# Weight rings in small blocks, sums of weights by transfers alone, and one more pair of seven products, in an encoder block

## The chip, the cores and the metric

The kernel runs on one core of a Trainium2 chip. The metric is the device time of one execution in microseconds. Engines are named as in the profile: PE (TensorE, with PEld its weight loads), DVE (VectorE), ACT (ScalarE), POOL (GpSimd) and SP (SyncE, which here only issues DMAs).

## The reference, cut to what matters

One layer of a bidirectional encoder over 256 tokens of width 2048, in float32:

```
h = rms_norm(x);  q, k, v of two attention branches, gates ga, gb = split(h @ w_in)
ya = windowed attention (8 query heads);  yb = dilated attention (12 heads in 3 groups, merged to 4)
merged = sigmoid(ga) * (ya @ w_branch_a) + sigmoid(gb) * (yb @ w_branch_b)
x = x + merged @ w_out
hf = rms_norm(x);  g = depthwise_conv3(hf @ w_ffn_gate)
x = x + (gelu(g) * (hf @ w_ffn_up)) @ w_ffn_down          # inner width 5632
x = x + sigmoid(rms_norm(x) @ w_ple_gate) * (p @ w_ple_proj)
out = rms_norm(x)
```

Nearly all of the work is the weight matrices, about 270 MB that are read once.

## The kernel before, in words

**Weights.** The weights lie in HBM as 258 pieces in the order of their use (`_pieces`), each 128 partitions by 16 blocks of 128 columns (1 MB). A piece goes by DMA on SP's queue into one of three `raw` buffers (`load`, L251). `produce` (L293) then splits a unit of it, mostly eight blocks (1024 columns), into two float32r parts: ACT copies it to `hi` (L310) and DVE subtracts, `lo = raw - hi` (L311). The parts stand in a ring of six buffers of eight blocks (`u`) or, for units that hold sums of weights, in a second ring of two (`v`). `drop` gives a buffer back when PE has used it, and `pump` produces the next units as long as a buffer is free. PE multiplies high and low parts in three passes (`thirds`, L413 to L415) or, where features are the output's partitions, in a 512-column and a 256-column pass (L356, L363).

**Stages.** A projects queries, keys and values and does the attention. B0 to B3 are the gates, each followed by the two branch projections `ba`, `bb`. D0 and D1 are the output projection. Then the MLP in two halves: E0 (gate and up), F00 and F01 (down), and the same as E1, F10 and F11. Last come the small projection `pp` and the gate G0, G2, G3. PE's program order follows the stages; a scheduler may move single instructions where nothing pins them.

**Quads.** B, D, F and G0 are made of pairs of 128-row chunks times two 512-column halves, for both 128-token halves (`quad_stage`, L420). A pair of kind `s` takes eight products of three matmuls each. Kinds `Z` and `S` take seven (Strassen's scheme in Winograd's form): PE accumulates M1 to M7 in seven PSUM banks, and DVE adds them up at a stage's end (`row_sums`, L910; the adds are L918 to L921). Seven products need four sums of the weights' quarters and four sums of the activations. The patterns are strings by stage: `GATES` for B0 to B3, `OUTS` for D, `DOWN` for the halves of F, `ALT` for G0.

For an `S` piece DVE makes all four sums of weights in the raw buffer (L289 and the two lines after it). For a `Z` piece one of the four is made ahead (`sum_ahead`, L263), in two halves of 256 columns: POOL's queue loads three quarters into spare space in SBUF (L269), DVE adds twice (L272, L273), POOL's queue stores the sum to HBM (L276). The piece is later loaded as three quarters (L255) and that sum (L256), and DVE makes the other sums (L283, L284). The stages' sums were spread by hand: 20 pieces for B and D in A (with spare space in the bias buffer `hb`), 12 for F0 in E0, 14 for F1 and G0 in E1. The DVE adds and POOL's transfers are pinned to program order (`keep`).

**Other names.** `rr` (L537) is the power on POOL that ends a norm's mean square; it stands in front of A's and of E0's sums in POOL's queue and near the end. `xr` holds the residual rows. L1016 multiplies a branch's sums into the gates, L998 takes the gates.

Of the kernel before, what the change touches and what calls it, by code (L numbers as in the profile page):

```python
# [2 lines left out]

# [165 lines left out]
def _unit_list():  # L169

    units, of = [], []
    for p, (kind, _) in enumerate(_PIECES):
        if p == 0:
            cuts = [("n", a * P, b * P) for a, b in ((0, 1), (1, 4), (4, 7), (7, 11), (11, PIECE))]
        elif kind == "Z":
            cuts = [("n", WIDE, 2 * WIDE), ("n", 2 * WIDE, 4 * WIDE), ("T21", 0, 2 * WIDE), ("T03", 2 * WIDE, 4 * WIDE)]
# [18 lines left out]
def _encoder(ctx: ExitStack, tc, xt, pt, xrow, cols, gainrow, table, onehot, mask, ident_in, wts, out):  # L195
# [55 lines left out]
    def load(r, a=0, b=PIECE):  # L251
        if a == 0:
            raws[r] = wpool.tile([P, PIECE * P], F32, name="raw", bufs=3)
        if _PIECES[r][0] == "Z":
# [1 line left out]
            nc.sync.dma_start(raws[r][:, :WIDE], ahead.pop(r))  # L256
# [4 lines left out]
    ahead = {}

    def sum_ahead(p, h, tag):  # L263

# [4 lines left out]
        keep(nc.gpsimd.dma_start(q, wts[p][:, :3 * WIDE].rearrange("p (q c) -> p q c", c=WIDE)[:, :, cols]))  # L269

        def add():
            keep(nc.vector.tensor_tensor(q[:, 0], q[:, 2], q[:, 0], op=ALU.subtract))  # L272
            keep(nc.vector.tensor_tensor(q[:, 0], q[:, 0], q[:, 1], op=ALU.add))  # L273
# [6 lines left out]
    def sums_of_weights(raw):  # L280

        q = [raw[:, i * WIDE:(i + 1) * WIDE] for i in range(4)]
        nc.vector.tensor_tensor(q[1], q[0], q[1], op=ALU.subtract)  # L283
        nc.vector.tensor_tensor(raw[:, 2 * WIDE:], raw[:, 2 * WIDE:], view(q[0], 0, (0, 2), (1, WIDE)), op=ALU.subtract)  # L284

    def all_sums_of_weights(raw):

        q = [raw[:, i * WIDE:(i + 1) * WIDE] for i in range(4)]
        nc.vector.tensor_tensor(raw[:, :2 * WIDE], raw[:, WIDE:3 * WIDE], raw[:, :2 * WIDE], op=ALU.subtract)  # L289
        nc.vector.tensor_tensor(q[2], q[2], q[0], op=ALU.subtract)  # L290
# [1045 lines left out]
```

## Time and profile before

| | us |
|---|---|
| median of three runs | 1455.06 (1453.43 to 1455.11) |
| profiled execution, its own time | 1453.29 |
| its span, first to last instruction | 1451.5 |
| PE busy | 1439.8 |
| DVE busy | 1255.9 |
| ACT busy | 836.3 |
| POOL busy | 126.7 |

The mean granted TensorE clock is 0.998. In the rows that follow, a group's row ends in its busy time, the mean duration of one instruction in ns and, behind the bar, the idle time of its engine just before them with what ended most of it. In a timeline a row has its start and its length in microseconds, and in brackets the idle time before it. A matmul's end is modelled and overlaps the next one's start, so the pace of PE is read from starts. In a DMA queue's row stand its packets, the MB moved, and the time of its packets as a share of 16 DMA engines; q1 is the queue that SP feeds, q0 that of POOL.

### The profile page before, as it was taken

The page shows a single profiled execution, that of the slowest core. Times are in us where ns is not written, and L with a number is a line of the kernel's source. Part 1 is how long each engine was busy: PE and PEld are TensorE (multiplying, and loading weights), DVE is VectorE, ACT ScalarE, POOL GpSimd, SP SyncE. Part 2 cuts the span into 40 slices and gives each one's busy share as a digit, 9 for nine tenths or more (in the row PEclk, how much of TensorE's full clock was granted, in tenths as well). Part 3 has the DMA queues.
Part 4 walks back from the last instruction along what each step waited for, and adds up shares of the span by engine and source line. Part 5 has one row for each costly group of instructions (what it writes and reads, how often), then busy time and mean ns, then how long its engine had stood idle before and what let it go on. Part 6 is the DMA issues. An engine that isn't in the chain of part 4 may idle for free.

```text
span 1451.5 us, 20060 instructions
## 1 busy us (share of the span) xinstructions
PE 1439.8 (99%) x7455; PEld 1231.0 (85%) x7455; DVE 1255.9 (87%) x1827; ACT 836.3 (58%) x1160; POOL 126.7 (9%) x193
## 2 busy tenths in 40 slices
PE   9999999999999999999999999999999999999997
PEld 8888888888888888788888888888888888888885
DVE  8778776779999999989787899997878799898994
ACT  7455544546656656666555566565545466564863
POOL 0112222210000000000222000000222200000000
PEclk9999999999999999999999999999999999999999
DMA  9776677764456466475777655566777765556462
GB/s 334 274 286 240 227 259 261 255 223 174 177 207 227 172 228 235 170 262 216 272 253 256 240 208 189 198 251 220 256 278 254 276 239 200 198 187 243 163 232 87
DMA packets 67805, 331.17 MB, mean 228 GB/s; under 512 B 8628, under 2 KB 13620, under 8 KB 41340
## 3 DMA queue, kind: packets, MB, share of 16 engines
q1 hardware_dynamic: 52268, 280.46, 53.7%
q0 software_dynamic: 14720, 48.25, 9.2%
q8 instruction: 58, 0.95, 0.3%
q10 hardware_dynamic: 720, 1.19, 0.2%
q14 instruction: 39, 0.32, 0.1%
HBM read 315.67 MB, written 14.20 MB: 227 GB/s over the span
## 4 chain that ended last, share of the span: by engine, by line
PE 92%; DVE 3%; issue 2%; DMA 1%; ACT 0%; POOL 0%; POOLq 0%; SPq 0%; DVEq 0%; ACTq 0%
PE bank L356 28%; PE bank L363 15%; PE bank L413 13%; PE bank L414 13%; PE bank L415 13%; PE bank L340 2%; PE bank L402 1%; PE bank L404 1%; PE bank L403 1%; PE bank L341 1%; DVE ul L311 1%; PE bank L966 1%; DMA raw<-in_wts 1%; DVE vl L311 1%; DMA xr<-in_xrow 0%
## 5 line engine op out<-in xcount | busy, mean ns | idle before, releaser
L310 ACT ACTIVATE uh<-raw 128x1024 fp32r<-128x1024 f32 (+2 forms) x519 | 515.4, 1007 | 293.1 <-PE bank L415 88.8
L311 DVE TENSOR_TENSOR ul<-raw,uh 128x1024 fp32r<-128x1024 f32 (+2 forms) x519 | 590.7, 1157 | 63.5 <-ACT uh L310 42.6
L356 PE MATMUL bank<-hf,uh 128*128 128x512 f32 x1408 | 336.6, 391 | 0.0
L356 PEld LDWEIGHTS bank<-hf,uh 128*128 128x128 f32 x1408 | 258.8, 188 | 50.6 <-DVE hf L522 0.4
L363 PEld LDWEIGHTS bank<-hf,ul 128*128 128x128 f32 x1408 | 180.7, 191 | 7.0
L363 PE MATMUL bank<-hf,ul 128*128 128x256 f32 x1408 | 183.3, 283 | 0.0
L310 ACT ACTIVATE vh<-raw 128x1024 fp32r<-128x1024 f32 x106 | 111.0, 1055 | 56.1 <-DVE raw L283 29.9
L311 DVE TENSOR_TENSOR vl<-raw,vh 128x1024 fp32r<-128x1024 f32 x106 | 127.3, 1217 | 1.7 <-ACT vh L310 0.5
L356 PE MATMUL bank<-hs,uh 128*128 128x512 f32 x432 | 103.6, 392 | 0.0
L356 PEld LDWEIGHTS bank<-hs,uh 128*128 128x128 f32 x432 | 79.5, 188 | 15.6
L414 PE MATMUL bank<-ul,act 128*128 128x512 f32 x218 | 84.8, 389 | 0.0
L415 PE MATMUL bank<-uh,act 128*128 128x512 f32 x218 | 84.8, 389 | 0.0
L413 PE MATMUL bank<-uh,act 128*128 128x512 f32 x218 | 84.5, 389 | 0.0
L505 ACT ACTIVATE t<-bank 128x256 f32<-128x256 f32 x122 | 45.4, 375 | 60.8 <-PE bank L363 50.1
L269 POOL DMA_DIRECT2D ahead<-in_wts x52 | 38.8, 747 | 378.5 <-DMA ahead<-ahead 209.3
L1112 ACT ACTIVATE gw<-gw,cl 128x256 f32<-128x256 f32 x44 | 24.1, 594 | 71.5 <-DVE gw L1109 71.4
L413 PE MATMUL bank<-uh,hs 128*128 128x512 f32 x154 | 60.8, 395 | 0.0
L272 DVE TENSOR_TENSOR ahead<-ahead 128x256 f32<-128x256 f32 x52 | 21.9, 422 | 44.7 <-DMA ahead<-in_wts 44.6
L415 PE MATMUL bank<-uh,hs 128*128 128x512 f32 x154 | 60.1, 390 | 0.0
L414 PE MATMUL bank<-ul,hs 128*128 128x512 f32 x154 | 60.0, 389 | 0.0
L363 PE MATMUL bank<-hs,ul 128*128 128x256 f32 x432 | 56.6, 284 | 0.0
L284 DVE TENSOR_TENSOR raw<-raw 128x1024 f32<-128x1024 f32 x46 | 56.0, 1217 | 0.3
(270 smaller groups left out, 2526.1 us busy)
## 6 DMA issues: line engine op xcount, KB each, us to landing
raw<-in_wts SPq DMA_DIRECT2D x205, 1024.0 KB, 4.9
raw<-in_wts SPq DMA_DIRECT2D x46, 768.0 KB, 4.6
ahead<-in_wts POOLq DMA_DIRECT2D x52, 384.0 KB, 5.1
hb<-in_wts POOLq DMA_DIRECT2D x40, 384.0 KB, 5.0
raw<-ahead SPq DMA_DIRECT2D x46, 256.0 KB, 4.9
ahead<-ahead POOLq DMA_DIRECT2D x52, 128.0 KB, 4.5
raw<-in_wts SPq DMA_DIRECT2D x12, 512.0 KB, 6.7
ahead<-hb POOLq DMA_DIRECT2D x40, 128.0 KB, 3.1
```

Of the source, the lines that this page charges most:

```text
L269: keep(nc.gpsimd.dma_start(q, wts[p][:, :3 * WIDE].rearrange("p (q c) -> p q c", c=WIDE)[:, :, cols]))
L284: nc.vector.tensor_tensor(raw[:, 2 * WIDE:], raw[:, 2 * WIDE:], view(q[0], 0, (0, 2), (1, WIDE)), op=ALU.subtract)
L310: nc.scalar.activation(hi, src, AF.Copy)
L311: nc.vector.tensor_tensor(lo, src, hi.bitcast(F32), op=ALU.subtract)
L340: nc.tensor.matmul(acc, hi[:, w], m, start=first, stop=False, skip_group_check=True)
L356: nc.tensor.matmul(acc, weights(u)[0][:, o * P:(o + 1) * P], m, start=first, stop=False, skip_group_check=True)
L363: nc.tensor.matmul(acc[:, T:], weights(u)[1][:, o * P:(o + 1) * P], m[:, :T], start=False, stop=last, skip_group_check=True)
L413: nc.tensor.matmul(acc, sh, wh, start=first, stop=False)
L414: nc.tensor.matmul(acc, sh, wl, start=False, stop=False)
L415: nc.tensor.matmul(acc, sl, wh, start=False, stop=last)
L505: keep(nc.scalar.activation(t, acc[:, T:], AF.Copy, scale=scale))
L1112: nc.scalar.activation(c[:, i], g[:, i], AF.Identity, scale=tap(1, f), bias=tap(3, f))
```

## The change

The three raw buffers become one tile of 48 blocks, and the two rings of split weights one queue of single blocks, first in first out: 48 blocks in the first store (`w`) and, from the end of the attention on, 16 more in a second (`v`). Loads are a list of steps of about half a piece, each issued as soon as enough blocks have been given back (`feed`), in groups of four at a time. A unit that does not lie in one run of blocks is split, and summed, run by run.

All `S` pieces become `Z`. A `Z` piece is now loaded as two sums from HBM (8 blocks) and three quarters (12 blocks), 20 blocks instead of 16. The two sums are made by four transfers between places in HBM on POOL's queue, two of which add while they write: quarter 0 is copied, quarter 1 added to it; the result is copied, quarter 3 added to that. DVE adds nothing for them and makes the other two sums in SBUF. The order of the seven products changes (M5 and M6, then M1, M2, M3, then M7, M4), with some signs. The steps for B are spread over A's jobs, those for D over B1 to B3, those for F and G0 over E0 and E1. In the second half of F the pattern has six `Z` in eleven instead of five. The ring of PSUM banks in E starts at another place.

The core of the diff (left out: signs, names, the list of first loads):

```diff
-GATES = ("sssssSSs", "ZsZZsSZs", "ZsZSsSZs", "ZsZSsSZs")
+GATES = ("sssssZZs", "ZsZZsZZs", "ZsZZsZZs", "ZsZZsZZs")
-DOWN = ("ZZsZsZsZsZs", "ZsZsZsZsZss")
-LASTS = 34
-ASK, ADD, STORE = 0, 12, 13
+DOWN = ("ZZsZsZsZsZs", "ZsZZsZsZsZs")
...
-            cuts = [("n", WIDE, 2 * WIDE), ("n", 2 * WIDE, 4 * WIDE), ("T21", 0, 2 * WIDE), ("T03", 2 * WIDE, 4 * WIDE)]
+            cuts = [(0, 8, 4), (8, 20, 8), (8, 16, 20)]
...
-RINGS = {"u": 6, "v": 2}
+STORE = {"w": 48, "v": 16}
+RAW = 48
...
+    def feed():
+        while state["load"] < len(loads):
+            step = loads[state["load"]]
+            if callable(step):
+                step()
+            else:
+                p, a, b = step
+                if len(rawfree) < b - a:
+                    break
+                if _PIECES[p][0] != "Z":
+                    load(p, a, b, wts[p][:, a * P:b * P])
+                elif a == 0:
+                    assert adding.pop(p) == 0
+                    load(p, a, b, ahead.pop(p))
+                else:
+                    load(p, a, b, wts[p][:, WIDE:])
+            state["load"] += 1
...
-        keep(nc.gpsimd.dma_start(q, wts[p][:, :3 * WIDE].rearrange("p (q c) -> p q c", c=WIDE)[:, :, cols]))
-        def add():
-            keep(nc.vector.tensor_tensor(q[:, 0], q[:, 2], q[:, 0], op=ALU.subtract))
-            keep(nc.vector.tensor_tensor(q[:, 0], q[:, 0], q[:, 1], op=ALU.add))
-        def store():
-            keep(nc.gpsimd.dma_start(ahead[p][:, cols], q[:, 0]))
+        def step(dst, src, op):
+            keep(nc.gpsimd.dma_start(dst, src, accum_op=op))
+            adding[p] -= 1
+        adding[p] = 4
+        return [partial(step, *e) for e in ((two, q[0], ALU.bypass), (two, q[1], ALU.add),
+                                            (three, two, ALU.bypass), (three, q[3], ALU.add))]
...
-        nc.vector.tensor_tensor(q[1], q[0], q[1], op=ALU.subtract)
-        nc.vector.tensor_tensor(raw[:, 2 * WIDE:], raw[:, 2 * WIDE:], view(q[0], 0, (0, 2), (1, WIDE)), op=ALU.subtract)
+        for o, op in ((8, ALU.subtract), (12, ALU.add)):
+            three, q = (runs_of(raws[p][i:i + 4]) for i in (4, o))
+            assert len(three) == len(q) == 1
+            three, q = (rawt[:, r[0][1] * P:(r[0][1] + 4) * P] for r in (three, q))
+            nc.vector.tensor_tensor(q, three, q, op=op)
...
+        cuts = sorted({r[2] for r in made[u][0]} | {r[2] for r in runs_of(raws[p][a:b])} | {b - a})
+        for o, e in zip(cuts, cuts[1:]):
+            hi, lo = part_of(u, o, e - o)
+            src = rawt[:, raws[p][a + o] * P:(raws[p][a + o] + e - o) * P]
+            nc.scalar.activation(hi, src, AF.Copy)
+            nc.vector.tensor_tensor(lo, src, hi.bitcast(F32), op=ALU.subtract)
...
-                    todo = (("M1", m1, 0, 0, 0), ("M7", sums[2], 2, 1, None), ("M6", sums[1], 2, 0, 2),
-                            ("M5", sums[0], 3, 0, None), ("M4", m4, 3, 1, 3),
-                            ("M2", m2, 1, 1, None), ("M3", sums[3], 1, 0, 1))
+                todo = (("M5", sums[0], 0, 0), ("M6", sums[1], 0, 1),
+                        ("M1", m1, 1, 0), ("M2", m2, 1, 1), ("M3", sums[3], 1, 2),
+                        ("M7", sums[2], 2, 0), ("M4", m4, 2, 1))
...
+    def spread_sums(pieces, slots):
+        last = len(slots) - 7
+        for e, p in enumerate(pieces):
+            first = e * last // max(len(pieces) - 1, 1)
+            for n, step in enumerate(sum_ahead(p)):
+                at(slots[first + 2 * n], step)
...
+    spread_sums(summed("B0", "B1", "B2", "B3"), slots[:-3])
+    spread_sums(summed("D0", "D1"), [("B%d" % j, i, 0) for j in range(1, 4) for i in range(8)])
...
-        turns["e"] = 0
-        todo = [(p, h) for p in sevens(half) for h in range(2)]
+        turns["e"] = 5 if half else 2
+        spread_sums(summed("F10", "F11", "G0") if half else summed("F00", "F01"),
+                    [(stage, i, 0) for i in range(1, len(jobs) - joint)])
```

More of the change, by code (lines that the diff above doesn't have):

```diff
@@ L280, in sums_of_weights @@
[L280 to L290, printed above, removed]
-        nc.vector.tensor_tensor(q[3], q[3], q[2], op=ALU.subtract)
+    made, taken, raws, left_of = {}, {}, {}, {}
@@ new lines, in _encoder, with extend, runs_of @@
+    state = {"unit": 0, "at": 0, "early": True, "load": 0}
+    store, free = {}, deque()
+    rawt = wpool.tile([P, RAW * P], F32, name="raw")
+    rawfree = deque(range(RAW))
+    loads = []
+    ahead, adding = {}, {}
+    def extend(which, pool):
+        store[which] = [pool.tile([P, STORE[which] * P], FR, name=which + half) for half in ("h", "l")]
+        free.extend((which, b) for b in range(STORE[which]))
+    extend("w", wpool)
+    def runs_of(blocks):
+        runs = []
+        for o, b in enumerate(blocks):
+            which, b = b if isinstance(b, tuple) else ("raw", b)
+            if runs and runs[-1][0] == which and runs[-1][1] + runs[-1][3] == b:
+                runs[-1][3] += 1
+            else:
+                runs.append([which, b, o, 1])
+        return runs
@@ new lines, in sum_of_weights, with part_of @@
+    def sum_of_weights(p):
+        for o, op in ((8, ALU.subtract), (12, ALU.add)):
[3 more added lines that the diff above has]
+            nc.vector.tensor_tensor(q, three, q, op=op)
+    def part_of(u, o, n):
+        runs, gone = made[u]
+        which, b, first, size = next(r for r in runs if r[2] <= o < r[2] + r[3])
+        assert gone <= o and o + n <= first + size
+        a = (b + o - first) * P
+        return [t[:, a:a + n * P] for t in store[which]]
@@ L308, in produce @@
-        hi = pool.tile([P, b - a], FR, name=ring + "h", bufs=RINGS[ring])
-        lo = pool.tile([P, b - a], FR, name=ring + "l", bufs=RINGS[ring])
-        nc.scalar.activation(hi, src, AF.Copy)
-        nc.vector.tensor_tensor(lo, src, hi.bitcast(F32), op=ALU.subtract)
-        if behind and u == _UNITS_OF[p][1]:
-            (sums_of_weights if _PIECES[p][0] == "Z" else all_sums_of_weights)(raw)
-        made[u] = (hi, lo)
+        p, a, b, done = _UNITS[u]
+        feed()
+        taken[u] = deque(free.popleft() for _ in range(b - a))
@@ L322, in pump, with weights, drop @@
                 break
             produce()
-    def weights(u):
+    def weights(u, o, n=1):
         while state["unit"] <= u:
             produce()
-        return made[u]
-    def drop(u):
-        del made[u]
-        state["u" if _UNITS[u][1] == "n" else "v"] += 1
+        return part_of(u, o, n)
+    def drop(u, n=None):
+        n = n or len(taken[u])
+        free.extend(taken[u].popleft() for _ in range(n))
+        made[u][1] += n
+        if not taken[u]:
+            del made[u], taken[u]
@@ L442, in cut @@
         def cut(u, i):
[L443 removed]
+            return weights(u, 4 * i, 4)
         for i, p in enumerate(pieces):
```

177 lines of the change are left out of this document (59 added, 118 removed).

## The prediction

> **What bounds the kernel now.** I read the page's totals first, then the busy time of each engine by stage, then the starts of single matmuls.
>
> ```profile
> span 1451.5 us, 20060 instructions
> PE 1439.8 (99%) x7455; PEld 1231.0 (85%) x7455; DVE 1255.9 (87%) x1827; ACT 836.3 (58%) x1160; POOL 126.7 (9%) x193
> ```
>
> PE is bound. By stage (columns: window, its length, then busy time and count of PE, PEld, DVE, ACT, POOL, the clock, the DMA share, GB/s), in the order A, B, D, first up and gate stage (E0), first down stage (F0), E1, F1:
>
> ```profile
> 60.00:320.00 260.00, 259.65 (x1469) 227.84 (x1468) 201.16 (x353) 135.79 (x219) 51.41 (x78) 1.00 0.72 257
> 330.00:545.00 215.00, 215.00 (x960) 176.83 (x959) 211.53 (x268) 132.48 (x153) 0.00 (x0) 1.00 0.55 201
> 545.00:625.00 80.00, 79.67 (x357) 64.65 (x356) 79.25 (x95) 51.58 (x63) 0.00 (x0) 1.00 0.60 211
> 640.00:860.00 220.00, 220.00 (x1266) 194.40 (x1264) 184.10 (x306) 124.84 (x186) 30.20 (x46) 1.00 0.70 246
> 870.00:990.00 120.00, 120.00 (x545) 99.38 (x544) 113.47 (x125) 68.29 (x77) 1.52 (x2) 1.00 0.59 217
> 1000.00:1225.00 225.00, 225.00 (x1296) 198.86 (x1295) 189.39 (x314) 126.30 (x187) 35.49 (x54) 1.00 0.69 247
> 1230.00:1340.00 110.00, 110.00 (x490) 90.97 (x489) 98.55 (x110) 64.45 (x74) 0.00 (x0) 1.00 0.57 212
> ```
>
> Between 60 and 1340 us PE shows 0.7 us idle (0.35 in A, 0.33 in D). DVE is the second engine: 98% busy in B, 99% in D, 95% in F0, but only 77 to 84% in A and in the E stages, where most of the adds for sums made ahead stand. So work taken from DVE pays only where DVE makes PE wait. A busy matmul overlaps the next, so small waits are read from starts. In D:
>
> ```profile
> 580.98 0.39 PE L415 MATMUL bank<-uh,merged 128*128 128x512 f32 x1
> ...
> 581.66 0.39 PE L415 MATMUL bank<-uh,merged 128*128 128x512 f32 x1
> 581.89 0.39 PE L413 MATMUL bank<-vh,S 128*128 128x512 f32 x1
> 582.58 0.50 PE L413 MATMUL bank<-vh,S 128*128 128x512 f32 x1 [0.30 <-DVE c L919]
> ```
>
> Three matmuls, one product of a quad, start 0.68 us apart (580.98 to 581.66), 0.227 each; 581.89 to 582.58 is 0.69 instead, so 0.46 us was lost to DVE. The other named wait is in A:
>
> ```profile
> 109.70 3.37 PE L356 MATMUL bank<-hs,uh 128*128 128x512 f32 x14
> 113.41 0.39 PE L711 MATMUL bank<-near,v 128*128 128x256 f32 x1 [0.35 <-DVE near L770]
> ```
>
> ```profile
> 108.93 0.42 DVE L272 TENSOR_TENSOR hb<-hb 128x256 f32<-128x256 f32 x1 [0.51 <-DMA hb<-in_wts]
> ```
>
> Fourteen matmuls at 0.227 end at 112.9, the next starts at 113.41: 0.5 us, with DVE having stood 0.51 us before it at an add whose data had not landed.
>
> **PE work.** Two pairs go from eight products to seven, one in each second-half down stage: 2 x 0.68 = **-1.36 us**. The seven S pieces that become Z stay at seven products. This term has no cover; PE is the bound.
>
> **DVE work.** Durations by shape:
>
> ```profile
> L311 DVE TENSOR_TENSOR ul<-raw,uh 128x1024 fp32r<-128x1024 f32 x461 | 554.5, 1218 | 60.7 <-ACT uh L310 40.1 <-issue 14.0 <-PE bank L363 6.1
> L284 DVE TENSOR_TENSOR raw<-raw 128x1024 f32<-128x1024 f32 x46 | 56.0, 1217 | 0.3
> L311 DVE TENSOR_TENSOR ul<-raw,uh 128x512 fp32r<-128x512 f32 x54 | 36.9, 683 | 1.5 <-ACT uh L310 1.5
> L283 DVE TENSOR_TENSOR raw<-raw 128x512 f32<-128x512 f32 x46 | 31.4, 684 | 0.3
> L272 DVE TENSOR_TENSOR ahead<-ahead 128x256 f32<-128x256 f32 x52 | 21.9, 422 | 44.7 <-DMA ahead<-in_wts 44.6
> L273 DVE TENSOR_TENSOR ahead<-ahead 128x256 f32<-128x256 f32 x52 | 21.6, 415 | 0.0
> L273 DVE TENSOR_TENSOR hb<-hb 128x256 f32<-128x256 f32 x40 | 16.8, 421 | 0.7
> L272 DVE TENSOR_TENSOR hb<-hb 128x256 f32<-128x256 f32 x40 | 16.8, 419 | 6.4 <-DMA hb<-in_wts 6.4
> ```
>
> Gone: the adds of L272 and L273 (77.1 us), the sums of L283 and L284 (87.4), and those of seven S pieces (one 1024 and two 512 wide each, 7 x 2.59 = 18.1). New: 110 sums 512 wide (75.2). The residues (`lo`) are cut where a ring wraps: 710 instructions for 621 in the built programs; a second half of a 1024 costs 2 x 683 - 1218 = 0.148 us more, 13 us; two pieces have 12 blocks more, 3 us. Net about -91 us of 1255.9. In B: ten Z at 1.90 - 1.37 and seven S at 2.59 - 1.37 give 5.3 + 8.5 = 13.8 us of 211.5, so DVE falls from 98 to about 92%. What that gives PE: the A wait goes with the adds that blocked DVE (-0.5). Of the 0.46 in D I take half (-0.2), since another bank is then waited for (below). Waits too short to show as idle, in D and at the head of E0, I put at -0.5, between 0 and -2. ACT issues 97 more instructions; even at a whole 0.63 us each,
>
> ```profile
> L310 ACT ACTIVATE uh<-raw 128x512 fp32r<-128x512 f32 x54 | 34.1, 631 | 51.7 <-DMA raw<-in_wts 17.2 <-PE bank L415 13.1 <-issue 12.3
> ```
>
> they are 61 us on an engine that is idle 38% or more of each window above.
>
> **The sums by transfers.** On POOL's queue at the start of stage A, before (`hb` is the staging space, `ahead` the stored sum):
>
> ```order
> L537 TENSOR_TENSOR rr<-rv,mhalf 128x4
> L269 DMA hb<-in_wts 128x3x256 x2
> L276 DMA ahead_628<-hb 128x256
> L269 DMA hb<-in_wts 128x3x256
> L276 DMA ahead_628<-hb 128x256
> ```
>
> and now (numbers are the pieces' sums):
>
> ```order
> L566 TENSOR_TENSOR rr<-rv,mhalf 128x4
> L306 DMA ahead_488<-in_wts 128x512
> L306 DMA ahead_489<-in_wts 128x512
> L306 DMA ahead_488<-in_wts 128x512
> L306 DMA ahead_489<-in_wts 128x512
> L306 DMA ahead_490<-in_wts 128x512
> L306 DMA ahead_488<-ahead_488 128x512
> ```
>
> Load, DVE add and store become four transfers a piece that wait only for one another. No engine paces them: POOL runs 108 of them (27 pieces, B and D) as fast as they land once its first power is done, and 112 (28 pieces) once its second, at E0's head, is. Their prices:
>
> ```profile
> q1 hardware_dynamic: 52268, 280.46, 53.7%
> ...
> ahead<-in_wts POOLq DMA_DIRECT2D x52, 384.0 KB, 5.1
> ahead<-ahead POOLq DMA_DIRECT2D x52, 128.0 KB, 4.5
> ```
>
> ```profile
> L256 SPq DMA_DIRECT2D raw<-ahead x46: 326/383/1393, 344.4 to 1371.5; - x46
> L537 POOL TENSOR_TENSOR rr<-rv,mhalf x3: 721/1018/1086, 53.1 to 1361.0; 128x2 f32<-128x2 f32 x2, 128x4 f32<-128x4 f32 x1
> ```
>
> The main queue moves 1 MB in 0.537 x 1451.5 / 280.46 = 2.78 us of all 16 DMA engines. A piece's four transfers write 1.05 MB and read 1.57 MB (an add reads its target too): 2.9 us of DMA if only the writes count, 4.4 if the reads do. No row shows an adding transfer; below 2.9 nothing argues for a gain. I take 4.4. One transfer lands in 4.5 to 5.1 us by the rows nearest in size, and each waits for the third before it, so one ends every 1.5 to 1.7 us: 108 are done 162 to 184 us after 54, by 240, and the first sum is loaded at 344. The 112 from 638 are done by 830; F0 begins at 870. So nothing waits for a sum: **0**. The cover is that distance; in A it holds for all 108 up to 2.7 us each.
>
> Raw loads share the DMA engines: 1.05 MB per 5.57 us in A and E is 2.92 us, 52%; 27 x 4.4 us in 186 us add 64%. That is over 100%, so sums spread out rather than raw loads, if raw loads are not held back. Two stretches of the DMA queues in A speak for that: POOL issued a load at 103.27, and from 103 to 106 the queues show
>
> ```profile
> q1 hardware_dynamic: 131, 0.98, 83.0%
> q0 software_dynamic: 12, 0.05, 4.0%
> ```
>
> ```profile
> 103.27 0.74 POOL L269 DMA_DIRECT2D hb<-in_wts  x1 [2.90 <-DMA ahead<-hb]
> ```
>
> The raw load, already in hand, went first and whole. [...]
>
> **Rings.** Raw loads of 1 MB become halves freed in blocks of four: earlier in A and E. A Z piece holds 20 raw blocks instead of 16, 0.26 MB x 55 = 14.4 MB more (5%), and its second load waits until its predecessors free 12. Split blocks of both stores form one queue of 64, where a quarter piece used to hold a whole buffer. These I set against each other: 0, between -1 and +2.
>
> **The order on PE.** A Z piece now begins with M5, whose bank DVE reads last at a stage's end; the scheduler moves it back. On PE where the first branch stage (`yb`, ending in M5's bank) meets the next quad stage, before:
>
> ```order
> L415 MATMUL bank_3682<-uh_3590,yb_3305 128x512
> L413 MATMUL bank_3721<-uh_3620,hs_95 128x512
> L414 MATMUL bank_3721<-ul_3621,hs_95 128x512
> L415 MATMUL bank_3721<-uh_3620,hs_95 128x512
> L413 MATMUL bank_3729<-vh_3636,S_3482 128x512
> ```
>
> and now (3332 is the branch's M5; 3373 is M6, 3380 M1, 3369 the new M5):
>
> ```order
> L450 MATMUL bank_3332<-wh_92,yb_3000 128x512
> L448 MATMUL bank_3373<-wh_92,S_3154 128x512
> L449 MATMUL bank_3373<-wl_93,S_3154 128x512
> L450 MATMUL bank_3373<-wh_92,S_3154 128x512
> L448 MATMUL bank_3380<-wh_92,hs_98 128x512
> L449 MATMUL bank_3380<-wl_93,hs_98 128x512
> L450 MATMUL bank_3380<-wh_92,hs_98 128x512
> L966 MATMUL bank_3384<-ident_75,c_3209 128x128
> L448 MATMUL bank_3391<-wh_92,hs_98 128x512
> L448 MATMUL bank_3369<-wh_92,S_3154 128x512
> ```
>
> M1 led and M5 came later still; M5 now comes seven matmuls and a transpose in, about 1.7 us after the branch's last. DVE's read in the trace:
>
> ```profile
> 367.10 0.39 PE L415 MATMUL bank<-uh,yb 128*128 128x512 f32 x1
> ```
>
> ```profile
> 370.55 0.68 DVE L1016 SCALAR_TENSOR_TENSOR c<-c,bank 128x512 f32<-128x512 f32 x1
> ```
>
> ```profile
> 583.64 0.68 DVE L921 TENSOR_TENSOR c<-bank,c 128x512 f32<-128x512 f32 x1
> ```
>
> M5 was free at 371.23, 3.9 us after the branch ended at 367.33: DVE was behind. With the same lag PE would lose 2.2 us here, and at D's middle 1.1 (free at 584.32; M5 now third there, 581.89 + 1.36 = 583.25) for the 0.46 before. With DVE at 92% instead of 98 a stage of some 57 us gives back about 3.5 us of lag, so I put the boundaries at 0.
>
> **Sum.** -1.36 - 0.5 - 0.2 - 0.5 = -2.56 us. The profiled execution took 1453.29 us (span 1451.5 and 1.8 around it); the median of the three runs is 1455.06, 1.8 above it. Taken from the median: **1452.5 us**. A measurement of this kernel can tell a change of about 0.2% (2.9 us) from none, so the forecast lies just inside that.
>
> **Rivals.**
> *The waits move to M5's bank.* DVE keeps its lag, since more blocks in one queue let it run further into work that is not urgent. Then 2.2 us at the first branch and 0.6 more in D, and about 0.5 at each of five like boundaries (three branches, two down stages): -2.36 + 2.2 + 0.6 + 2.5 = +2.9, 1458 us. For it: DVE's 3.9 us above; against it: 91 us less work.
> *Contention, slower.* The unpaced transfers hold raw loads back in A after 54 us and in E0 after 638. Raw needs 52%; it decides from the point where POOL takes more than 48% for longer than the three pieces in the raw ring (16.7 us of PE work) cover. If raw gets 45%, a piece takes 2.92 / 0.45 = 6.5 us instead of 5.57 over 27 x 4.4 / 0.55 = 216 us, so 33 pieces x 0.92 = 30 less 16.7, 14 us, twice: +28 - 2, 1481 us. For it: no engine paces POOL, and the price of an adding transfer is unseen. Against it: the raw load that went first at 103.27, and a DMA share of 0.72 in A now without a wait on raw that PE shows.
> *All small waits go.* DVE is never late again in B, D and F: the hidden waits give 3 instead of 0.5 and D its whole 0.46: -5.3, 1449.8 us.
> That the transfers make no sums ahead at all is no rival: the program holds 220 of them.
>
> **How the numbers follow.** Forecast 0.56 (between -1 and -4.5, which splits into 0.31 faster by more than 0.2% and 0.25 within it), small waits gone 0.08 (faster), waits at M5 0.20 (0.13 within, 0.07 slower), contention 0.16 (slower): faster 0.39, same 0.38, slower 0.23. The range goes from 1449 (all small waits) to 1465 (waits at M5, and the first third of contention); above it I leave about 0.1, below it 0.06.
>
> **What would show it.** Right: 5,003 matmuls of 512 columns and no change of the 0.227 us step; DVE near 1165 us; no idle at 113 and less than 0.5 us around 582; POOL's transfers over by about 240 and 830 us; PE not waiting for raw weights in A or E0. Wrong: PE idle in A beyond 0.35 us with ACT waiting for raw loads that land later than 8 us after issue (contention); PE released by the DVE lines that read M5 (L921, L1016) for a microsecond or more at stage starts (waits moved); sums that land so late that SP stands before a load from `ahead`.

## The result, and the profile after

The changed kernel took 1510.12 us (median of 4 runs, 1507.16 to 1513.6) beside 1454.24 us of the kernel before on the same chip: a ratio of 1.0385, 95% interval 1.0359 to 1.0412, so 3.9% slower. The forecast was 1452.5 us with a range of 1449 to 1465. The totals of the page of the changed kernel:

```profile
span 1506.4 us, 20758 instructions
PE 1458.2 (97%) x7449; PEld 1236.3 (82%) x7449; DVE 1183.6 (79%) x1741; ACT 856.0 (57%) x1257; POOL 157.3 (10%) x229
```

PE has the six matmuls less that were forecast (7449 for 7455), DVE is 72 us lighter, and the span is 55 us longer. By stage (columns as in the prediction; A, then D with E0's head, E0, F0):

```profile
60.00:320.00 260.00, 255.92 (x1436) 224.96 (x1435) 170.97 (x265) 131.16 (x214) 71.49 (x104) 0.99 1.00 281
545.00:640.00 95.00, 88.30 (x383) 69.62 (x382) 79.72 (x100) 52.54 (x68) 0.00 (x0) 0.98 0.64 218
640.00:860.00 220.00, 216.68 (x1235) 189.95 (x1235) 174.64 (x293) 134.35 (x222) 43.85 (x63) 1.00 0.93 264
870.00:1010.00 140.00, 124.13 (x538) 99.10 (x537) 97.69 (x122) 64.41 (x78) 31.63 (x46) 0.94 0.92 260
```

PE, which stood idle for 0.7 us between 60 and 1340 us before, now stands idle in A, around D's end, a little in E0 and above all in F0. The DMA share is 1.00 in A (0.72 before) and 0.92 in F0 (0.59 before). In D it is only 0.64, and PE stands idle there too: one cause alone will not do. PE's own pauses, from its timeline (start, length, in brackets the idle time and its releaser):

```profile
111.72 1.52 PE L391 MATMUL bank<-hs,wh 128*128 128x512 f32 x6
117.33 0.58 PE L719 MATMUL bank<-near,v 128*128 128x256 f32 x1 [4.08 <-DVE near L778]
...
592.31 0.39 PE L450 MATMUL bank<-wh,merged 128*128 128x512 f32 x1
596.02 0.50 PE L448 MATMUL bank<-wh,S 128*128 128x512 f32 x1 [3.32 <-DVE c L921]
...
597.53 0.63 PE L450 MATMUL bank<-wh,merged 128*128 128x512 f32 x1
597.96 0.63 PE L448 MATMUL bank<-wh,S 128*128 128x512 f32 x1
...
964.66 0.40 PE L450 MATMUL bank<-wh,ends 128*128 128x512 f32 x1
969.34 0.80 PE L448 MATMUL bank<-wh,S 128*128 128x512 f32 x1 [4.28 <-ACT wh L339]
```

The place that lost 0.46 us before (D0 to D1) now loses 3.5 (592.31 to 596.02, less 0.227). After the pause the matmuls start 0.43 us apart instead of 0.227 (597.53 to 597.96), and the clock column of the windows says why:

```profile
597.20:600.20 3.00, 3.00 (x9) 2.32 (x8) 3.00 (x4) 1.23 (x2) 0.00 (x0) 0.50 1.03 427
972.00:979.00 7.00, 6.25 (x15) 4.41 (x15) 7.00 (x12) 3.34 (x4) 1.65 (x2) 0.50 0.97 245
```

The granted clock is 0.50 there. The trace's clock records show half the clock for 27.3 us in all between 60 and 1400 us, and for none of the kernel before in that time; the 60 matmuls started in these stretches that did not also wait took 9.2 us more than their usual steps. The stretches last 3.41, 6.83 and 10.24 us. In the 3.41 us from 112.32 us PE was busy for 0.92 us, in those from 593.61 us for 1.00 us, and a stretch at half the clock began behind both; in the 3.41 us from 433.20 us it was busy for 1.84 us, and the clock stayed at 1.00.

To add pauses up I take, for each matmul, the time to the next one's start less 0.227, 0.120 or 0.109 us by its shape, and count what is over 0.04 us (slow matmuls of a halved clock are in it), over the whole execution. That gives 12.3 us before and **67.9 us after**. 1451.5 - 1.4 for the products + 55.6 = 1505.7 us, and the span is 1506.4: the pauses are the whole loss.

What ACT and DVE waited for, before and then after:

```profile
ACT uh L310 <- DMA raw<-in_wts: 54.3, 46, 5.1
```

```profile
ACT wh L339 <- DMA raw<-in_wts: 96.2, 59, 9.2
...
ACT vh L339 <- DMA raw<-in_wts: 29.9, 14, 3.8
...
DVE wl L340 <- ACT wh L339: 115.7, 88, 8.4
```

Raw data is late (126 us of waiting for 54), and DVE stands at `lo` behind ACT (115.7 us, 42.6 before). PE's own longest waits, after:

```profile
PE bank L449 <- DVE wl L340: 8.2, 7, 1.6
PE bank L448 <- ACT wh L339: 7.4, 5, 4.3
PE bank L448 <- DVE c L921: 5.5, 3, 3.3
PE bank L719 <- DVE near L778: 4.1, 1, 4.1
```

So PE stands first of all for the split weights themselves (L340, L339); the adds that it also waits for (L921, L778) are queued behind splits on DVE. The DMA queues between 60 and 300 us, before and after:

```profile
q1 hardware_dynamic: 7709, 43.13, 51.0%
q0 software_dynamic: 5841, 19.14, 21.6%
...
raw<-in_wts SPq DMA_DIRECT2D x38, 1024.0 KB, 5.0
```

```profile
q0 software_dynamic: 10800, 25.27, 50.9%
q1 hardware_dynamic: 13324, 42.05, 49.2%
...
raw<-in_wts SPq DMA_DIRECT2D x74, 512.0 KB, 8.4
ahead<-in_wts POOLq DMA_DIRECT2D x74, 256.0 KB, 8.8
```

With both queues busy each took about half of the time there (between 700 and 830 us, in E0, it is 55.0% for q1 and 41.3% for q0), a raw load of half the size landed in 8.4 us for 5.0, and a sum's transfer in 8.8 us. So POOL's transfers end late. On POOL's timeline stand the last of A's, one pair of E0's (the last for F0 and the first for F1) and the very last:

```profile
324.58 0.81 POOL L306 DMA_DIRECT2D ahead<-in_wts  x1 [5.49 <-DMA ahead<-ahead]
...
823.59 1.36 POOL L306 DMA_DIRECT2D ahead<-in_wts  x2 [5.33 <-DMA ahead<-ahead]
...
988.04 0.80 POOL L306 DMA_DIRECT2D ahead<-in_wts  x1 [6.56 <-DMA ahead<-ahead]
```

Their last packets end at 330 us in A and at 994 us after E0. Yet no load waited for a sum: no row of SP's waits names a transfer that writes `ahead`.

### The profile page after: what moved, and what is told of

The parts are those of the page before. It is cut to its first block, busy times and chain, and to the rows that moved or that the text cites. A ratio compares the mean times of both kernels' runs of the same rounds, so it can differ in the third digit from the quotient of the medians.

```text
span 1506.4 us, 20758 instructions
## 1 busy us (share of the span) xinstructions
PE 1458.2 (97%) x7449; PEld 1236.3 (82%) x7449; DVE 1183.6 (79%) x1741; ACT 856.0 (57%) x1257; POOL 157.3 (10%) x229
## 4 chain that ended last, share of the span: by engine, by line
PE 39%; DMA 7%; DVE 6%; issue 2%; ACT 1%; POOL 0%; POOLq 0%; DVEq 0%; ACTq 0%
PE bank L391 20%; PE bank L398 11%; DMA raw<-in_wts 7%; DVE wl L340 3%; PE bank L448 3%; PE bank L449 3%; PE bank L450 3%; ACT wh L339 1%; DVE vl L340 1%; DVE raw L318 1%; DMA raw<-ahead 1%; PE bank L966 0%; ACT vh L339 0%; DVE c L919 0%; DVE xr L1033 0%
## 5 line engine op out<-in xcount | busy, mean ns | idle before, releaser
L340 DVE TENSOR_TENSOR wl<-raw,wh 128x1024 fp32r<-128x1024 f32 (+3 forms) x546 | 576.6, 1080 | 199.9 <-ACT wh L339 115.7
L339 ACT ACTIVATE wh<-raw 128x1024 fp32r<-128x1024 f32 (+3 forms) x546 | 506.9, 944 | 369.5 <-PE bank L391 118.7
L391 PE MATMUL bank<-hf,wh 128*128 128x512 f32 x1056 | 256.5, 391 | 1.3 <-DVE c L921 1.3
L391 PEld LDWEIGHTS bank<-hf,wh 128*128 128x128 f32 x1056 | 194.1, 188 | 39.2 <-DVE c L921 1.7
L340 DVE TENSOR_TENSOR vl<-raw,vh 128x512 fp32r<-128x512 f32 (+2 forms) x174 | 155.5, 911 | 26.3 <-ACT vh L339 16.2
L339 ACT ACTIVATE vh<-raw 128x512 fp32r<-128x512 f32 (+2 forms) x174 | 136.2, 804 | 59.2 <-DMA raw<-in_wts 29.9
L398 PEld LDWEIGHTS bank<-hf,wl 128*128 128x128 f32 x1056 | 137.0, 191 | 5.2
L398 PE MATMUL bank<-hf,wl 128*128 128x256 f32 x1056 | 140.8, 283 | 0.0
L391 PE MATMUL bank<-hs,wh 128*128 128x512 f32 x432 | 103.6, 392 | 0.0
L448 PE MATMUL bank<-wh,act 128*128 128x512 f32 x209 | 82.9, 399 | 1.8 <-ACT wh L339 1.7
L450 PE MATMUL bank<-wh,act 128*128 128x512 f32 x209 | 82.6, 395 | 0.0
L448 PE MATMUL bank<-wh,S 128*128 128x512 f32 x118 | 48.8, 415 | 12.6 <-ACT wh L339 5.7
```

Source lines behind the costliest of these rows:

```text
L339: nc.scalar.activation(hi, src, AF.Copy)
L340: nc.vector.tensor_tensor(lo, src, hi.bitcast(F32), op=ALU.subtract)
L391: nc.tensor.matmul(acc, weights(u, o)[0], m, start=first, stop=False, skip_group_check=True)
L398: nc.tensor.matmul(acc[:, T:], weights(u, o)[1], m[:, :T], start=False, stop=last, skip_group_check=True)
L448: nc.tensor.matmul(acc, sh, wh, start=first, stop=False)
L450: nc.tensor.matmul(acc, sl, wh, start=False, stop=last)
```

## The experiments

Two causes suggested themselves: contention (C) and the rings with the order on PE (R). All ratios are to the kernel before, on the same chip; "pauses" are summed as above, in the one execution that was profiled (in e1 and e11 the slowest, 5 and 9 us above the median). The rows come from several chips, on which the kernel before took 1454.1 to 1455.6 us, and the four runs of e9 alone go from 1472.2 to 1480.9 us. So a difference between two rows holds to some 2 to 4 us.

| kernel | us | ratio, 95% interval | pauses |
|---|---|---|---|
| the change | 1510.12 | 1.0385 [1.0359, 1.0412] | 67.9 |
| e1 no transfers | 1484.28 | 1.0194 [1.0175, 1.0214] | 49.0 |
| e2 copies only | 1498.19 | 1.0303 [1.0288, 1.0318] | 57.4 |
| e3 bb's second bank M4 | 1513.82 | 1.0411 [1.0395, 1.0426] | 75.3 |
| e4 E1's transfers held | 1498.04 | 1.0304 [1.0278, 1.0331] | 49.2 |
| e5 = e1, 16 raw blocks more | 1458.94 | 1.0026 [1.0016, 1.0036] | 19.3 |
| e6 = e1, 8 split blocks less | 1485.29 | 1.0210 [1.0191, 1.0229] | 45.5 |
| e7 = e1, other banks | 1484.60 | 1.0200 [1.0183, 1.0217] | 44.2 |
| e8 = e1, 16 of 20 blocks loaded | 1476.04 | 1.0142 [1.0120, 1.0164] | 36.6 |
| e9 change, 16 raw blocks more | 1478.91 | 1.0152 [1.0125, 1.0179] | 38.5 |
| e10 = e9, E1's transfers held | 1475.19 | 1.0135 [1.0112, 1.0158] | 28.5 |
| e11 = e10, yet more raw | 1474.94 | 1.0123 [1.0094, 1.0152] | 35.3 |
| e12 before, one pair more | 1463.98 | 1.0062 [1.0042, 1.0083] | 23.5 |
| e13 = e10, padded tiles | 1471.71 | 1.0117 [1.0103, 1.0132] | 24.4 |
| e14 = e9, paced transfers | 1471.98 | 1.0120 [1.0105, 1.0134] | 31.5 |
| e15 change, paced transfers | 1498.55 | 1.0305 [1.0287, 1.0323] | 56.4 |
| e16 before, the pair later | 1464.53 | 1.0069 [1.0057, 1.0081] | 24.3 |
| e17 = e14, no tile moved | 1468.03 | 1.0092 [1.0077, 1.0107] | 28.9 |
| e18 = e9, unused tiles | 1482.90 | 1.0197 [1.0179, 1.0214] | 33.7 |

Five of these sums by stage (A from 60 to 325 us, B to 545, D to 640, E0 to 865, F0 to 1010; a slow kernel's stages begin some us late in them):

| kernel | A | B | D | E0 | F0 | rest |
|---|---|---|---|---|---|---|
| before | 2.5 | 1.3 | 2.5 | 0.3 | 0.3 | 5.4 |
| the change | 8.4 | 4.9 | 11.3 | 5.0 | 26.4 | 11.9 |
| e1 | 1.9 | 9.5 | 15.2 | 6.1 | 3.4 | 12.9 |
| e5 | 1.9 | 3.6 | 5.6 | 1.1 | 0.0 | 7.1 |
| e17 | 1.8 | 14.0 | 4.0 | 2.7 | 0.0 | 6.4 |

**Transfers taken away, made cheaper, held back.** e1 leaves the transfers out (a Z piece's first eight blocks then come from the weights, so its sums are others than the reference's):

```diff
     def spread_sums(pieces, slots):
+        return
...
-                    load(p, a, b, ahead.pop(p))
+                    load(p, a, b, wts[p][:, :2 * WIDE])
```

> The rings, the patterns and the order of the change, but POOL makes no sums: the first two blocks of four of a Z piece are loaded straight from the weights, so SP's traffic and all work on DVE, ACT and PE stay and only the 220 transfers are left out (the sums are then not the reference's). Theory C (contention: the transfers hold raw loads back in A, in E0 and in F0): the 26 us that PE loses between 916 and 1010 us, the 6 us in A and most of the 16 us between 596 and 670 go; 1465 to 1472 us. Theory R (rings and order: 20 raw blocks for a Z piece of 48, and M5's bank first): the losses stay where they are; 1500 us or more.

e2 makes the adding transfers plain copies (the adds are left out):

```diff
-        ... (two, q[1], ALU.add), ... (three, q[3], ALU.add)
+        ... (two, q[1], ALU.bypass), ... (three, q[3], ALU.bypass)
```

> All 220 transfers stay, but the 110 that add are plain copies (the sums are then not the reference's). Theory C with the price in the adding: a piece's four transfers cost about 3.1 us of DMA instead of 5.1, the last of E0's come before F0 begins, and the loss in F0 shrinks from 26 us to under 8; 1482 to 1490 us. Theory C with the price in the number of transfers and their landing: under 6 us of gain, 1504 us. Theory R: no change, 1510 us.

e4 lets POOL wait, ahead of the transfers for F1 and G0, for values of `xr` that F0 writes last:

```diff
+        if half:
+            g = sc.tile([P, 2], F32, name="hold_on", bufs=1)
+            keep(nc.vector.tensor_scalar(g, xr[:, :, D - 1], 0.0, 1.0, op0=ALU.mult, op1=ALU.add))
+            h = sc.tile([P, 2], F32, name="held_on", bufs=1)
+            keep(nc.gpsimd.tensor_tensor(h, g, mhalf[:, :2], op=ALU.pow))
         spread_sums(summed("F10", "F11", "G0") if half else summed("F00", "F01"),
```

> The 64 transfers for F1 and G0 wait on POOL for a power of a value that DVE takes from the residual rows after F0's end, so that they run in E1 and none runs in F0. Theory C: PE's loss in F0 (26 us) falls to under 5 and E1 takes the transfers without loss, 1484 to 1488 us. Theory R: the loss in F0 stays, 1508 to 1512 us.

e1 came out between the theories: the transfers cost 26 us, and 30 us stay without any. By stage the transfers' part lies in F0 and in A; in E0, where they run from 668 us on, the pauses are no fewer without them. Of the 26 the adding itself is 12 (e2, whose time lies in none of its three ranges). With the hold F0 is nearly clear of pauses:

```profile
870.00:1010.00 140.00, 137.36 (x641) 113.03 (x640) 114.35 (x145) 78.07 (x96) 0.00 (x0) 1.00 0.59 199
```

PE is busy for 137.4 of 140 us there (124.1 in the change), at a DMA share of 0.59. So transfers that run into F0 do harm there; but e4 gained only 12 us where its pauses fell by 18.7, which stayed unexplained until e18.

**The order on PE.** e3 gives the second branch stage M4's bank in place of M5's; e7 turns the banks in D1, F01 and F11, so that M5, which now comes first, uses the bank that is read first.

```diff
-  ("bb%d" % j, yb.get, ("M7", "M5"))
+  ("bb%d" % j, yb.get, ("M7", "M4"))
```

> The second branch sum stands in M4's bank instead of M5's, so that the bank that DVE frees last at a branch's end is the one that the next stage needs last. Theory R: the 1.25 us at 376 and the 2.1 us at 433 to 436 go, 1506 to 1507 us. Theory C: DVE is late there because weights were late, and PE waits a little later for the weights instead; 1509 to 1510 us.

```diff
+        turn = {"M5": "M1", "M1": "M7", "M7": "M5"} if stage in ("D1", "F01", "F11") else {}
...
-                accs[name] = bank(name)
+                accs[name] = bank(turn.get(name, name))
```

> The kernel without transfers (1484.28 us) with other PSUM banks in D1, F01 and F11: M5 there uses the bank of M1 (read first at a stage's end), M1 that of M7, M7 that of M5. O (order) expects the waits on L921 at 596, 960 and 1320 us to go with the slow matmuls behind them: 1472 to 1476 us. D and H expect that the other adds are as late, so a part at most: 1478 to 1485 us.

Neither gained (1513.82 for 1510.12; 1484.60 for 1484.28). PE's longest pauses in D end with L921, but that add is late with all that stands beside it; which bank comes first decides little.

**The rings.** The largest part of the 30 us is around D. In e1 at D's middle, on PE, DVE and ACT:

```profile
590.67 0.39 PE L449 MATMUL bank<-wh,merged 128*128 128x512 f32 x1
595.88 0.79 PE L447 MATMUL bank<-wh,S 128*128 128x512 f32 x1 [4.82 <-DVE c L921]
...
586.32 1.76 DVE L339 TENSOR_TENSOR wl<-raw,wh 128x1536 fp32r<-128x1536 f32 x1 [3.72 <-ACT wh L338]
588.00 0.68 DVE L918 TENSOR_TENSOR c<-c,bank 128x512 f32<-128x512 f32 x1
...
595.14 0.68 DVE L921 TENSOR_TENSOR c<-bank,c 128x512 f32<-128x512 f32 x1
...
584.80 1.49 ACT L338 ACTIVATE wh<-raw 128x1536 fp32r<-128x1536 f32 x1 [3.46 <-DMA raw<-in_wts]
```

ACT stands 3.46 us for raw data, DVE 3.72 for ACT, and the adds that free M5's bank stand behind. Three experiments on e1 (with what it leaves out) tell why the data is late. e5 adds a second raw tile of 16 blocks after the attention and takes 8 split blocks for it (left out below: the helper that finds a block in either tile); e6 takes the 8 split blocks alone; e8 loads only 16 of a Z piece's 20 blocks (four keep old data) but holds 20.

```diff
-STORE = {"w": 48, "v": 16}
+STORE = {"w": 48, "v": 8}
+MORE = 16
...
+        more.append(held["tok"].tile([P, MORE * P], F32, name="more"))
+        rawfree.extend(range(RAW, RAW + MORE))
```

> The kernel without transfers (1484.28 us; a Z piece's first eight blocks come from the weights, so the sums are not those of the reference) with 16 raw blocks more (64 instead of 48, from the end of the attention on) and 8 blocks less of split weights (56 instead of 64). Theory D (depth): a Z piece holds 20 raw blocks, 48 are 2.4 pieces, loads are issued too late, ACT and DVE stand for raw data, and the adds that free PSUM banks stand behind them. D expects 1462 to 1472 us and little DVE waiting for ACT waiting for raw data around 580 to 640 us. Theory H (head of line): the single queue of split blocks lets splits stand ahead of urgent adds; H expects the same time as with 8 split blocks less alone. Theory O (order): M5 first meets the bank that is read last; O expects no change, 1482 to 1487 us.

```diff
-STORE = {"w": 48, "v": 16}
+STORE = {"w": 48, "v": 8}
```

> The kernel without transfers (1484.28 us) with 8 blocks less of split weights (56 instead of 64 from the end of the attention on) and nothing else. H (head of line: fewer splits stand ahead of urgent adds) expects 1465 to 1476 us. D (depth of the raw ring) expects no gain or a loss, 1484 to 1490 us, since the weights in hand become fewer. O (order) expects no change, 1482 to 1487 us.

```diff
-        for _, at_, o, n in runs_of(mine[a:b]):
+        for _, at_, o, n in runs_of(mine[a:b][n0:]):
...
-                    load(p, a, b, wts[p][:, :2 * WIDE])
+                    load(p, a, b, wts[p][:, :2 * WIDE], 4)
```

> The kernel without transfers (1484.28 us) where a Z piece still holds 20 raw blocks but only 16 are loaded (four of the first eight keep what stood there, so the products are not those of the reference either). If the bytes are what makes raw data late, 1464 to 1474 us; if it is the places in the ring (D), 1480 to 1486 us; H and O expect no change.

e5 gave 25.3 us, more than any theory asked, e6 nothing, e8 8.2, between its two ranges. So it is the depth of the raw ring; a fifth less to load for a Z piece gives a third as much as the depth. Splits that stand ahead are not it, as far as 8 blocks less of them can tell. ACT's waits for raw data, in e1 and in e5:

```profile
ACT wh L338 <- DMA raw<-in_wts: 78.8, 57, 4.6
ACT vh L338 <- DMA raw<-in_wts: 25.0, 15, 3.4
```

```profile
ACT wh L346 <- DMA raw<-in_wts: 10.1, 14, 2.4
ACT vh L346 <- DMA raw<-in_wts: 5.1, 3, 3.4
ACT wh L346 <- DMA more<-in_wts: 4.4, 2, 3.9
```

104 us became 20, and in e5's DVE timeline the same add comes 11 us earlier (5 of which e1 had lost ahead of D), and PE has no pause there:

```profile
584.00 0.68 DVE L931 TENSOR_TENSOR c<-bank,c 128x512 f32<-128x512 f32 x1
```

(L931 is L921 with ten lines more above it.) **Both causes together.** e9 is the whole change with e5's edit, e10 that with e4's hold, e11 that with 64 raw blocks from the start:

> The changed kernel (1510.12 us) with 16 raw blocks more from the end of the attention on and 8 blocks less of split weights, all else as it is, transfers too. Theory D+C (two causes that add: a raw ring too shallow for pieces of 20 blocks, and transfers that hold raw loads back): the depth gives its 25 us here too, 1482 to 1488 us. Theory D>C (the transfers hurt only because the ring is shallow, so that a later landing is not covered): 1460 to 1472 us. Theory C>D (under the transfers depth gives nothing since the DMA engines are full): 1500 to 1510 us.

> As the kernel before it in this row of runs, and the transfers for F1 and G0 held back until F0 is over. D+C: 1472 to 1478 us, 10 to 12 below the one without the hold. D>C: no more than 4 us below it, 1458 to 1468 us.

```diff
-STORE = {"w": 48, "v": 8}
-RAW = 48
+STORE = {"w": 40, "v": 8}
+RAW = 64
```

> As the kernel with the hold, with 64 raw blocks from the start and 80 from the end of the attention on, and 40 (then 48) blocks of split weights instead of 48 (then 56). D: the wait at 117 us in A goes, and a few us more, 3 to 8 us below the one with the hold. If the blocks of split weights are what is short now, the same or slower by 1 to 5 us.

The depth gives 31.2 us here, and the time is a little under the range of "two causes that add", as if a deep ring covered some of the contention too. The hold on top (e10) took 10.0 us of pauses away but gave only 3.7 us of time, which is within e9's own spread; a longer step between matmuls, below, takes 8 us. e11 missed: it gained nothing, and A's pause grew from 6.2 to 9.1 us. ACT still waited for raw data there (12.6 us between 60 and 120 us, 17.3 in e10), so depth did not help in A, where the DMA share is 0.99 in e9; that e11 also has 8 split blocks less was not tried by itself. Against full DMA engines, e14 and e15 pace the transfers: POOL waits, ahead of each piece's four, for a small DVE instruction at that place in the program.

```diff
+    def not_before():
+        g = sc.tile([P, 16], F32, name="hold_on", bufs=2)[:, :2]
+        keep(nc.vector.tensor_scalar(g, mhalf[:, :2], 0.0, 1.0, op0=ALU.mult, op1=ALU.add))
+        h = sc.tile([P, 16], F32, name="held_on", bufs=1)[:, :2]
+        keep(nc.gpsimd.tensor_tensor(h, g, mhalf[:, :2], op=ALU.pow))
...
+            at(slots[first], not_before)
             for n, step in enumerate(sum_ahead(p)):
```

> The changed kernel with 16 raw blocks more (1478.91 us), and each piece's four transfers wait on POOL for a small DVE instruction at the place in the program where they were written, so that they are spread over A, B, E0 and E1 instead of running as fast as they land. Theory D+C: both causes are then treated, the wait at 120 us and the losses in F0 go, 1456 to 1463 us. If transfers cost by their bytes wherever they stand, 1472 to 1480 us.

> The changed kernel (1510.12 us) with the paced transfers alone, raw ring as it is (48 blocks). D+C: what the kernel without transfers took, 1480 to 1488 us. If a shallow ring suffers from spread transfers too (in B and D there were none before), 1490 to 1505 us.

Neither reached its lower range: 7 us gained on the deep ring, 11.6 on the shallow one. e14 stands at the edge of what "transfers cost by their bytes wherever they stand" expects.

**The step between matmuls.** In every kernel with extra small tiles the sum of pauses falls short of the span: e10's is 1451.5 - 1.4 + 16.2 = 1466.3 by the pauses and 1474.3 by the trace. The missing 8 us are in the step. e13 pads e10's two tiles to 64 bytes; e17 lets e14's pacing work in `warm`, which stands already; e18 gives e9 two tiles that nothing uses.

```diff
-            g = sc.tile([P, 2], F32, name="hold_on", bufs=1)
+            g = sc.tile([P, 16], F32, name="hold_on", bufs=1)[:, :2]
```

> The kernel with 16 raw blocks more and the hold (1475.19 us), its two small tiles for the hold 64 bytes a partition each instead of 8. With the hold as it was, matmuls of 512 columns started 229 to 231 ns apart from 300 us on (227 to 228 without it), some 8 us in all. If the 16 bytes by which they shifted all later tiles are the cause, the pace is 227 to 228 again and the time 1464 to 1469 us. If the pace has another cause (another chip, the transfers' place), no change, 1473 to 1478 us.

```diff
-        g = sc.tile([P, 16], F32, name="hold_on", bufs=2)[:, :2]
+        state["paced"] = n = state.get("paced", -1) + 1
+        g, h = warm[:, n % 3:n % 3 + 1], warm[:, 3:]
...
```

> The kernel with 16 raw blocks more and paced transfers (1471.98 us), its pacing instructions working in a tile that stands already and is used no more, so that no later tile moves in SBUF (its own two tiles moved them by 192 bytes). Its 512-column matmuls started 228.5 to 229.5 ns apart from 300 us on, against 227 to 228.4 in the kernel with 16 raw blocks more alone. If the addresses are the cause: 227 to 228.4 again, 1464 to 1467 us. If not: 229 and 1470 to 1474 us.

```diff
+            for name in ("hold_on", "held_on"):
+                sc.tile([P, 2], F32, name=name, bufs=1)
```

> The kernel with 16 raw blocks more (1478.91 us) and two tiles of 8 bytes that nothing uses, where the hold had its own; they move later tiles by 64 bytes and change nothing that is computed or transferred. If the addresses set the slower step: 229 to 230 ns from 300 us on, 1484 to 1490 us. If it is the hold or its place: 227 to 228.4 ns, 1474 to 1482 us.

From 300 us on the mean step of 512-column matmuls (those under 0.24 us) is 227.6 ns before, 227.7 in e9 and 227.6 in e17, but 229.9 in e10 and e18. In B, the first and the last row of stretches without a pause, e9 (50 matmuls) and e18 (49):

```profile
519.81 0.39 PE L458 MATMUL bank<-wh,S 128*128 128x512 f32 x1
...
530.91 0.39 PE L456 MATMUL bank<-wh,hs 128*128 128x512 f32 x1
```

```profile
519.69 0.39 PE L456 MATMUL bank<-wh,hs 128*128 128x512 f32 x1
...
530.82 0.39 PE L456 MATMUL bank<-wh,hs 128*128 128x512 f32 x1
```

11.10 / 49 = 0.2265 us and 11.13 / 48 = 0.2319 us, at a granted clock of 1. Two tiles that nothing uses cost that. They move every later tile by 64 bytes a partition (not 16, as e13's expectation has it); 64-byte padding, which moves them by 128, does not cure it (e13, 229 ns), no move at all does (e17). The times of e17 and e18 lie beside the ranges set for them; it is the step that tells. PE's matmuls run in the same order in e9, e10 and e18; some instructions of DVE and ACT do not, but in e17 far more of them are moved, so the addresses are the likelier cause; which tile matters was not tried. Free of this, pacing is worth 10.9 us (e9 to e17): PE is busy throughout A, and in F0 for 140.00 of 140 us. What is left of e17 stands where D's sums now run, in B:

```profile
60.00:320.00 260.00, 260.00 (x1475) 228.51 (x1474) 175.98 (x288) 135.47 (x219) 58.41 (x85) 1.00 0.87 248
400.00:500.00 100.00, 93.55 (x398) 75.63 (x397) 83.91 (x114) 54.50 (x70) 28.76 (x32) 0.95 0.93 281
```

**The two products alone.** e12 and e16 add the sixth pair of seven to the kernel before, as fourth or as eighth pair of the stage.

```diff
-DOWN = ("ZZsZsZsZsZs", "ZsZsZsZsZss")
+DOWN = ("ZZsZsZsZsZs", "ZsZZsZsZsZs")
```

> The kernel before (1454.24 us) with one edit: one more pair of seven in each second-half down stage, its sums of weights made as that kernel makes them. The product term of the prediction alone: two products of three matmuls of 0.227 us, -1.4 us, 1452.5 to 1453.2 us; with DVE late in F for two pieces more with four sums, 1453 to 1456 us.

```diff
-DOWN = ("ZZsZsZsZsZs", "ZsZsZsZsZss")
+DOWN = ("ZZsZsZsZsZs", "ZsZsZsZZsZs")
```

> The kernel before (1454.24 us) with a sixth pair of seven in each second-half down stage as the eighth pair rather than the fourth (ZsZsZsZZsZs). If the 1463.98 us of the other place came from the sums of activations that are late at the start of the stage (6.9 us at 1237), that goes: 1452.5 to 1455 us. If DVE has no room for the sums of weights of two pieces more, 1458 us and above.

Both lost some 10 us, so it is not the place. In e12 PE stands at the start of F1, where 7 of its 11 us of further pauses are, for `pair`, the last activations of E1 that DVE reads out of PSUM:

```profile
1234.06 0.39 PE L415 MATMUL bank<-vh,ends 128*128 128x512 f32 x1
1236.91 0.49 PE L413 MATMUL bank<-uh,ends 128*128 128x512 f32 x1 [2.46 <-DVE pair L509]
...
1239.78 0.77 PE L413 MATMUL bank<-uh,S 128*128 128x512 f32 x1 [1.53 <-DVE pair L509]
```

The pattern's new end, `Zs` for `ss`, needs sums of the last activations; DVE makes them, with some of the splits, ahead of this read. Then the matmuls start 0.43 us apart (1241.20 to 1241.63), their step at a clock of 0.50 in the change. The change has no such pause at its F1; that fits its lighter DVE, but its rings and its order differ too, and nothing took them apart.

## Why the prediction was wrong

**The sums by transfers, put at 0: the step that failed first.** The price of a piece was nearly right: 0.189 x 1506.4 / 55 = 5.2 us of DMA, 4.4 taken. That was an estimate by the bytes read, which no run shows by themselves; in the trace the packets of the two copies took 1.5 us and those of the two adds 3.6. Its bytes and the 52% of the raw loads were known to be over 100%. What failed is the sentence after: "sums spread out rather than raw loads, if raw loads are not held back", and the landing time of 4.5 to 5.1 us, taken from rows with half-empty queues. Raw loads were held back (8.4 us for 5.0 in A) and the transfers landed in 8.8. They ended at 330 us instead of 240, and at 994 (from 668 on) instead of 830 (from 638 on). That nothing would wait for a sum came true; the harm was done to the raw loads.

The stretch from 103 to 106 us, where a raw load seemed to go first and whole, was too little to go by, and misread: POOL's loads issued at 99.05 and 110.15 us had their first packet 1.44 us after the issue, the one issued at 103.27 us had it at 105.75, 2.48 us after. So its packets came about 1 us later than by the other two; for the rest of that stretch they were not yet there. And in the trace after, with POOL's transfers running throughout, raw loads did not go first: between 60 and 300 us the two queues took 50.9 (q0) and 49.2% (q1) of the time.

The rival "contention" had the mechanism. Its price, +28, is close to the 25.8 measured (the change less e1), but by luck: it put 14 us each into A and E0, and the pauses that go in e1 are 6.5 us in A, none in E0 and 23 in F0, by transfers for F1 that ran on into it, which was in no case. The 45% that it left the raw loads was an estimate; the trace shows 49.2% for q1 in A and 55.0% in E0.

**The rings, put at 0, between -1 and +2: the second step that failed,** and as large: 25 us without the transfers, 31 with them (e5, e9). "20 raw blocks instead of 16" was counted as 5% of bytes. It had to be read as time in hand: a Z piece lasts 21 x 0.227 = 4.8 us, 48 blocks are 2.4 such pieces or 11.4 us, and blocks come back in fours only as DVE has split them; against that stand 5.3 us of landing (the median of the 512-KB loads in e1 between 560 and 660 us) and the splits behind it (1.49 us on ACT and 1.76 on DVE for 1536 columns at D's middle in e1). Before, three pieces of 16 stood in hand.

**The boundaries, put at 0.** What the first rival named (waits on L921 and L1016) came, with 3.5 instead of 0.6 us in D, but as a symptom: other banks change nothing (e3, e7), a deeper raw ring removes it.

**What no case held:** that pauses cost more than themselves. About 9 of the 56 us (9.2 in the trace) are matmuls at a granted clock of 0.50.

**What held.** Two products less are six matmuls less, -1.4 us in the account of pauses, though in the kernel before they would not have come free (e12). DVE's work fell: its instructions' durations add up to 1292.2 us for 1378.6 before, 86 us less where 91 were forecast (its busy time, in which they overlap, fell by 72 to 1183.6, not to 1165). The wait behind DVE's adds in A is gone where nothing else is in the way: in e1 and e17 PE is busy for 260.00 of 260 us.

**The account.** From the change at 1510.1: deeper raw ring -31.2 (e9), paced transfers -10.9 (e17), no transfers -9.1 (e5, 1458.9), each to some 2 to 4 us, and in this order: without the transfers the ring is worth 25.3. What then stays, 0.26% over the kernel before, is 7 us of pauses, none over 1.3 us, most of them in B and around D, less 1.4 for the products; it was not taken apart. No version tried beats the kernel before.

## What to carry to other kernels

Read a ring's depth as time: blocks in hand divided by what the hungriest step eats, against the landing time plus the engines in between. Here a piece that takes 20 places for 16 was given 64 blocks for 48, and that was worth 25.3 us without the transfers (e5) and 31.2 with them (e9). Transfers that no engine paced took 50.9% of the DMA time between 60 and 300 us and landed in 8.8 us instead of 4.5 to 5.1, so price a transfer by its landing under load, and pace it if what it shares with is needed sooner. An early wait showed up as a late instruction somewhere else (at D's middle in e1 ACT's 3.46 us for raw data and DVE's 3.72 us for ACT, ahead of an add for which PE stood 4.82 us): experiments on a line that PE waits for found nothing, the one on what ACT and DVE waited for found the cause.

## What the runs showed of the hardware

- In the trace of the change the granted clock was 0.50 in five stretches between 60 and 1400 us (from 115.73 us for 6.83 us, from 597.01 for 3.41, from 931.51 for 3.41, from 969.06 for 10.24, from 1006.61 for 3.41), in that of the kernel before in none. In the 3.41 us ahead of each, PE was busy (as the views count it) for 0.92, 1.00, 1.01, 0.00 and 1.79 us. Of two pauses of like length, 3.32 us of idle PE before 596.02 us in the change were followed by such a stretch; 3.25 us before 591.21 us in e7 were not (clock 1.00 from 591.2 to 596.2). In these stretches the 512-column step was 0.427 us, for 0.227 at a clock of 1.00.
- In the change the 110 adding transfers moved in 14,080 packets of 2,048 bytes, 178 ns each in the median, and the 110 plain copies, of the same size, in 7,040 packets of 4,096 bytes, 159 ns each: 0.087 and 0.039 ns a byte, more than twice the time.
- Two tiles of 8 bytes that nothing uses made the step of 512-column matmuls 2.2 ns longer from 300 us on (229.9 in e18, 227.7 in e9), by this some 8 us in the whole kernel; why is open.
